# Contracting the 64-row products over 128 rows, with zeros in the others

## The chip, the cores and the metric

One core of a Trainium2 chip runs the whole step. The metric is the device time of one execution in microseconds (us). Engines are named as in the profile: PE (TensorE, its matmuls), PEld (its weight loads), DVE (VectorE), ACT (ScalarE), POOL (GpSimd), SP (SyncE, which issues nearly all DMAs).

## The reference

One layer over 2048 frames of a new stream (the prompt) and 64 frames of a running stream (the sample). An input projection feeds eight heads of banded attention and four heads of a gated linear recurrence; both are gated, joined, projected out and normalized. Cut to what the change touches:

```python
def sample_attention(q, k, v, ck, cv, rel_bias):      # 64 frames, 512 cached keys
    kk = jnp.concatenate([ck, k], axis=1)[:, None]    # 512 + 64 keys
    vv = jnp.concatenate([cv, v], axis=1)[:, None]
    ...
    return band_attention(q[:, None], kk, vv, rel, valid, rel_bias)[:, 0]

def band_attention(q, k, v, rel, valid, rel_bias):
    ...
    p = jax.nn.softmax(s, axis=-1).astype(v.dtype)
    return jnp.einsum('bnhqk,bnkhd->bnqhd', p, v)     # contracts over the keys

def step(S, inp):                                     # the recurrence, block by block
    ...
    A = jnp.where(mask, jnp.einsum('bthk,bshk->bhts', qt, kt), 0.0)
    o = jnp.einsum('bthk,bhkv->bthv', qt, S) + jnp.einsum('bhts,bshv->bthv', A, vb)
    S = jnp.exp(bl)[..., None] * S + jnp.einsum('bshk,bshv->bhkv', kb * jnp.exp(bl[:, None] - b), vb)
    return S, o
```

The sample has 64 frames. So its attention has 512 + 64 keys, and its recurrence has one chunk of 64 frames, where the prompt has chunks of 128.

## The kernel before

The frames are worked in four super-blocks (`SUPER`) of 512, 576, 512 and 512 columns; the second has the sample's 64 frames behind its 512 of the prompt. In each, PE runs 32 projections (`project`, tiles acc). Between their matmuls, in steps of two, the program lays the matmuls of the attention and of the recurrence as they become ready.

What sets the order: every engine is an in-order queue that the program fills itself. The class `Plan` keeps a clock of planned times; generators (threads) wait on planned times, on tokens for buffers (`tk`), or on conditions, and `mm`, `C.act`, `C.dve`, `C.pool` and `C.dma` advance the plan. What a generator emits between two waits goes to the engines' queues at that place.

Four heads pairs (`pair_jobs`, `attention`) handle the attention, two heads each. Keys lie on the partitions for the product with v: tile v has nine key tiles of 128 rows; the ninth (index 8) holds the sample's own 64 keys, in rows 0 to 63. For the sample, `sample_a` takes the scores, turns the probabilities to keys on partitions (tile tr), splits them into a high and a low part (tile ph, two buffers, `split_p`: ACT casts, DVE subtracts) and multiplies with v: for each of two heads four products over 128 cached keys (tile vc, in the buffer wraw) and one over the 64 last keys, j = 4.

The recurrence (`rec_block`, four heads) works in chunks of 128 rows, and of 64 for the sample (`chunks`, entry smp, two sub-blocks of 32). Of each chunk: A (tile asb, masked), kn (keys turned to frames on partitions, tile k1; for two heads of the later super-blocks by DMA, `by_dma`, L1518 to 1528, else by PE's transposes, L1530 to 1540), the products kv = kn with iv (L1545) and og = iv with A plus the state's part (L1580). iv is tile gi, [128, 640], filled by ACT from a DMA (`ev_i`); the sample's chunk is columns 512 to 639, rows 0 to 63. The last chunk's products contract over `w` = 64 rows.

Of float32 products (kv, og) each is two MATMUL instructions in the trace; the pv products take float32r tiles and are one each. All go through the helper `mm` (L249).

Of the kernel before, what the change touches and what calls it, by code (L numbers as in the profile page):

```python
# [17 lines left out]
P = 128  # L18
# [3 lines left out]
DEC = 64  # L22
WIN = 512
# [14 lines left out]
SUPER = [  # L38
# [4 lines left out]
]  # L43
# [140 lines left out]
def hymba_step(  # L184
# [26 lines left out]
    pool = nc.gpsimd  # L211
# [14 lines left out]
    def T(pool_, shape, dt, tag, **kw):  # L226
        uid[0] += 1
        return pool_.tile(list(shape), dt, tag=tag, name=f"{tag}_{uid[0]}", **kw)
# [13 lines left out]
    def f32(ap):  # L242
        return ap.bitcast(F32)
# [4 lines left out]
    def mm(out, w, x, n, slow=False, **kw):  # L248
        pe.matmul(out, w, x, **kw)  # L249
        C.mm(n, slow)  # L250

    def transpose(out, x, idn):
# [4 lines left out]
                                     w=WBUFS, raw=RAWB, xn=XNB, kv0=1, kv1=1, rec=1, sga=2, bias0=1, bias1=1, gf=1, gi=1, gg=1,  # L257
# [471 lines left out]
    room = {}  # L729
# [29 lines left out]
    def pair_jobs(sb, p):  # L759
# [12 lines left out]
        def open_(h):  # L772

            yield from tk[f"kv{h}"].get()
            if "kd" not in room:
                room["kd"] = T(pa, [P, 2, WIN + NMAX], F32R, "kd")
                room["v"] = T(pa, [P, 2, 9, 2, 64], F32R, "v")
                room["q"] = T(pa, [P, 2, QW], F32R, "q")
            d.kd, d.v, d.q = room["kd"], room["v"], room["q"]
            if sb:  # L780
                cd = carry[sb - 1][p]
                sp.dma_start(f32(d.kd[:, h, 0:512]), cd[:, h])
                d.k_t[h] = C.dma(256)
                sp.dma_start(f32(d.v[:, h, 0:4].rearrange("p t s d -> p (t s d)")), cd[:, 2 + h])
                d.v_t[h] = C.dma(256)
            d.open[h] = True
            C.spawn(load_bias(sb, p, d, h), 1)
# [185 lines left out]
    def vcols(v, t, h, rows):  # L973
        return (v[:rows, h, t] if v is room["v"] else v[:rows, t, 2 * h : 2 * h + 2, :]).rearrange("p s d -> p (s d)")

    def split_p(pt, ph, krows, wid, t):
        act.copy(ph[:krows, 0, :wid], pt[:krows, :wid])  # L977
        t = C.act(wid, t)
        yield "D", t
        dve.tensor_sub(ph[:krows, 1, :wid], pt[:krows, :wid], f32(ph[:krows, 0, :wid]))  # L980
        return C.dve(wid, t)
# [179 lines left out]
    def sample_a(d, c0, marks):  # L1161
        yield lambda: d.left == [1, 1]
        yield lambda: d.cache is not None and all(x >= c0 + DEC for x in d.q_n + d.k_n + d.v_n)
        yield "D", max(d.q_t + d.k_t + d.v_t)
        q, kd, v, p = d.q, d.kd, d.v, d.p
        kc, vc = d.cache


        spans = [(kc, 0, 512), (kd, 512 + c0, DEC)]

        z = c0 + DEC
        for part in (q, ql):
            dve.memset(f32(part[:, :, z : z + DEC]), 0.0)
            dve.tensor_copy(part[:, 1, z + DEC : z + 2 * DEC], f32(part[:, 1, c0:z]))
        t = C.dve(500)
        yield t
        yield from tk["s_ps"].get()
        yield from tk["pr"].get()
        sps = s_ps()
        for i, (ks, k0, kn) in enumerate(spans):  # L1180
            for part in (q, ql):
                for h in range(2):
                    a = (c0, z)[h]
                    mm(sps[:, i, :kn], part[:, h, a : a + P], ks[:, h, k0 : k0 + kn], kn,
                       start=part is q and h == 0, stop=part is ql and h == 1)
        t = C.pe()
        yield "D", t
        s = T(wk, [P, 640], F32, "pr", bufs=PRB)
        nm = T(wk, [P, 2], F32, "nm", bufs=4)
        for h in range(2):  # L1190
            hs = own[h]
            for i, kn in enumerate((512, DEC)):
                dve.tensor_tensor_reduce(s[hs, i * 512 : i * 512 + kn], sps[hs, i, :kn],
                                         d.bias[hs, h, 64 * h + i * 512 : 64 * h + i * 512 + kn],
                                         1.0, 3e38, ALU.add, ALU.min, nm[hs, i : i + 1])
                t = C.dve(kn, t)
        dve.tensor_tensor(nm[:, 0:1], nm[:, 0:1], nm[:, 1:2], ALU.min)
        t = C.dve(10, t)
        tk["s_ps"].put(1, t)
        for h in range(2):  # L1200
            d.left[h] -= 1
            tk[f"bias{h}"].put()
        yield "A", t
        out = []
        yield from softmax_exp(s, nm, 576, out, t)
        pr, t = out[0]
        yield lambda: marks[-1]["pv"] and turn["ph"] == turn["given"]
        yield t + 300.0
        phs = []
        for j0, nj, kr in ((0, 4, P), (4, 1, DEC)):  # L1210
            yield from tk["tr"].get()
            pt = tr_ps()
            for j in range(j0, j0 + nj):
                transpose(pt[:kr, (j - j0) * P : (j - j0 + 1) * P], pr[:, j * P : j * P + kr], ident)
            t = C.pe()
            if j0:
                tk["pr"].put(1, t)
            yield "A", t
            yield from tk["ph"].get()
            ph = T(wk, [P, 2, 512], F32R, "ph", bufs=2)  # L1220
            t = yield from split_p(pt, ph, kr, nj * P, t)
            tk["tr"].put(1, t)
            phs.append(ph)
        yield t + 200.0
        yield from tk["mixa"].get()
        mix = T(wk, [P, 256], F32, "mixa", bufs=2)
        yield from tk["pv"].get()
        pv = psum("pv").rearrange("p (h s q) -> p h s q", h=2, s=2)[:, :, :, :DEC]
        for h in range(2):
            for j in range(5):  # L1230
                kr = P if j < 4 else DEC
                cc = (j % 4) * P + h * DEC
                mm(pv[:, h], vcols(vc, j, h, kr) if j < 4 else vcols(v, 4 + c0 // P, h, kr), phs[j // 4][:kr, :, cc : cc + DEC], P,
                   start=(j == 0), stop=(j == 4))
        tk["ph"].put(2, C.pe())
        t = C.pe()
        yield "A", t
        for h in range(2):
            t = yield from finish_pv(h, pv[:, h], mix, DEC, t)
        tk["pv"].put(1, t)  # L1240
        tk["raw"].put(2)
        C.spawn(mix_out(d, mix, c0, DEC, t, True), 1)
# [5 lines left out]
    def head_jobs(sb, h):  # L1248
# [65 lines left out]
        def ifree():  # L1314
            if r.gi is None:
                if tk["gi"].n == 0:
                    return False
                tk["gi"].take()
                r.gi = True
                r.iv = T(pg, [P, 5 * P], F32, "gi")  # L1320
            return True

        def qd():
# [38 lines left out]
    def rec_block(r, off, bn, lastb):  # L1362
# [77 lines left out]
        A = asb  # L1440
# [75 lines left out]
        if by_dma:  # L1516
            yield ta + 200.0
            yield lambda: "t" in rows  # L1518
            yield rows["t"]
            kn = tmp("k1").rearrange("p (c t) -> p c t", t=P)  # L1520
            if nprc:
                act.copy(kn[:, :nprc].rearrange("p c (a j) -> p c a j", j=32),
                         kh[:, :full].rearrange("p (a c j) -> p c a j", a=4, j=32))
            if bn > full:
                act.copy(kn[:DEC, nprc], kh[:DEC, full : full + P])
            t = C.act(bn, rows["t"])
            yield t + 200.0
        else:
            yield max(ta, tkh) + 200.0
            tg = bank()  # L1530
            for i, (cc, nbk, smp) in enumerate(chunks):
                w = nbk * 32
                transpose(tg[:w, i], kh[:, cc : cc + w], ident)
            t = C.pe()
            yield "A", t
            kn = tmp("k1").rearrange("p (c t) -> p c t", t=P)
            for cs, w in merged():
                act.copy(kn[:w, cs], tg[:w, cs])
            t = C.act(bn, t)
            yield t + 200.0  # L1540
        kv = bank()
        iv = r.iv
        for i, (cc, nbk, smp) in enumerate(chunks):
            w = nbk * 32
            mm(kv[:, i], kn[:w, i], iv[:w, off + cc : off + cc + P], P, True, start=True, stop=True)  # L1545
        t = C.pe()
        yield "D", t
        before = []
# [28 lines left out]
        og = bank()  # L1577
        for i, (cc, nbk, smp) in enumerate(chunks):
            w = nbk * 32
            mm(og[:, i, :w], iv[:w, off + cc : off + cc + P], A[:w, i, :w], P, True,  # L1580
               start=True, stop=before[i] is None)
            if before[i] is not None:
                mm(og[:, i, :w], before[i], qh[:, cc : cc + w], P, True, start=False, stop=True)
# [673 lines left out]
```

## Time and profile before

| | |
|---|---|
| time, median of three runs | 1241.81 us (1240.01 to 1243.0) |
| the profiled execution's own time | 1241.93 us |
| its span, first to last instruction | 1240.2 us |
| mean granted clock of PE in it | 0.999 |
| instructions in it | 21233 |

How to read the rows that follow in the prediction. A group row has the line, engine, operation, tiles (out<-in, without buffer numbers), for PE the active rows*columns of the array, the shape and the count; then busy time in us, mean length of one in ns, and the engine's idle time ahead of them with what ended it. A timeline row has the start and length in us of a run of equal instructions, merged with their count. The ends of matmuls are modelled, so what a matmul holds PE for is read from one start to the next. A line of waits has the time in total, how often, and the longest.

### The profile page before, as it was taken

The page shows a single profiled execution, that of the slowest core. Times are in us where ns is not written, and L with a number is a line of the kernel's source. Part 1 is how long each engine was busy: PE and PEld are TensorE (multiplying, and loading weights), DVE is VectorE, ACT ScalarE, POOL GpSimd, SP SyncE. Part 2 cuts the span into 40 slices and gives each one's busy share as a digit, 9 for nine tenths or more (in the row PEclk, how much of TensorE's full clock was granted, in tenths as well). Part 3 has the DMA queues.
Part 4 walks back from the last instruction along what each step waited for, and adds up shares of the span by engine and source line. Part 5 has one row for each costly group of instructions (what it writes and reads, how often), then busy time and mean ns, then how long its engine had stood idle before and what let it go on. Part 6 is the DMA issues. An engine that isn't in the chain of part 4 may idle for free.

```text
span 1240.2 us, 21233 instructions
## 1 busy us (share of the span) xinstructions
PE 1228.5 (99%) x7398; PEld 1078.9 (87%) x7398; DVE 893.8 (72%) x1897; ACT 680.3 (55%) x1526; POOL 417.3 (34%) x702
## 2 busy tenths in 40 slices
PE   9999999999999999999999999999999999999997
PEld 7888888999999999998888888988888888788786
DVE  7687878777767677687587667785768566867775
ACT  6354546655565547574465556664646445644443
POOL 7665565111120111201242242133342202665543
PEclk9999999999999999999999999999999999999999
DMA  8897979667575476555787878678888686988431
GB/s 339 302 319 256 328 281 343 205 179 242 159 221 156 150 238 210 193 167 187 265 270 253 300 241 282 227 238 276 261 275 262 222 251 212 336 260 252 131 136 68
DMA packets 158324, 294.36 MB, mean 237 GB/s; under 512 B 51657, under 2 KB 98377, under 8 KB 140554
## 3 DMA queue, kind: packets, MB, share of 16 engines
q1 hardware_dynamic: 157784, 292.74, 70.7%
q8 instruction: 58, 0.95, 0.3%
q14 instruction: 48, 0.39, 0.1%
q10 hardware_dynamic: 434, 0.27, 0.1%
HBM read 198.52 MB, written 95.49 MB: 237 GB/s over the span
## 4 chain that ended last, share of the span: by engine, by line
PE 90%; DMA 5%; DVE 2%; ACT 1%; SPq 1%; issue 0%; POOL 0%; ACTq 0%; DVEq 0%; POOLq 0%
PE acc L249 58%; PE g L249 9%; PE pv L249 7%; PE tr L253 6%; PE s L249 5%; PE tr L249 4%; DMA vT<-way 2%; DMA w<-wd 2%; DMA way<-vT 1%; DMA out_dram<-ck 1%; PE g L253 1%; DMA bias<-wind 0%; DVE pr L948 0%; SPq L711 0%; SPq L1684 0%
## 5 line engine op out<-in xcount | busy, mean ns | idle before, releaser
L249 PE MATMUL acc<-xh,w 128*128 128x512 f32 (+2 forms) x2720 | 564.5, 347 | 0.6 <-ACT xh L409 0.5
L249 PEld LDWEIGHTS acc<-xh,w 128*128 128x128 f32 x2720 | 435.7, 189 | 51.5 <-ACT xh L409 0.9
L249 PE MATMUL acc<-xl,w 128*128 128x512 f32 (+2 forms) x1360 | 291.4, 346 | 0.2 <-DVE xl L415 0.2
L249 PEld LDWEIGHTS acc<-xl,w 128*128 128x128 f32 x1360 | 220.5, 189 | 26.2 <-DVE xl L415 0.4
L948 DVE CUSTOM_DVE_ANT_0 pr<-s,bias 128x640 f32<-128x640 f32 (+4 forms) x128 | 94.2, 736 | 53.6 <-PE s L249 53.1
L965 ACT ACTIVATE pr<-pr,nm 128x640 f32<-128x640 f32 (+4 forms) x132 | 100.3, 760 | 52.8 <-DVE nm L948 52.5
L977 ACT CAST ph<-tr 128x512 fp32r<-128x512 f32 (+3 forms) x176 | 87.8, 506 | 74.5 <-PE pv L249 45.5
L473 POOL TENSOR_TENSOR w<-wraw,w 128x256 fp32r<-128x256 f32 x120 | 102.3, 881 | 55.6 <-DVE w L468 40.5
L980 DVE TENSOR_TENSOR ph<-tr,ph 128x512 fp32r<-128x512 f32 (+3 forms) x176 | 100.7, 587 | 21.6 <-ACT ph L977 21.0
L249 PE MATMUL pv<-ph,v 128*128 128x256 f32 (+2 forms) x344 | 97.8, 371 | 0.9 <-DVE ph L980 0.6
L253 PE MATMUL tr<-ident,pr 128*128 128x128 f32 x580 | 88.2, 273 | 0.5 <-DVE sm L968 0.5
L1596 POOL TENSOR_TENSOR k<-ob 128x512 f32<-128x512 f32 (+2 forms) x20 | 18.0, 902 | 200.3 <-ACT ob L1587 162.3
L510 POOL TENSOR_TENSOR xn<-wraw,xn 128x256 fp32r<-128x256 f32 x48 | 40.6, 848 | 132.1 <-ACT xn L507 127.1
L1121 POOL TENSOR_TENSOR mixa<-mixa,sga 128x256 f32<-128x256 f32 (+1 forms) x36 | 28.6, 793 | 167.9 <-DVE mixa L1019 142.2
L969 DVE TENSOR_SCALAR pr<-pr,sm 128x640 f32<-128x640 f32 (+4 forms) x132 | 76.2, 577 | 4.7
L1019 DVE TENSOR_TENSOR mixa<-mixa,pv 64x256 f32<-64x256 f32 (+1 forms) x144 | 56.8, 394 | 31.0 <-ACT mixa L1015 27.3
L253 PEld LDWEIGHTS tr<-ident,pr 128*128 128x128 f32 x580 | 69.8, 140 | 10.3 <-PE tr L253 0.9
L575 ACT ACTIVATE sig<-acc 128x512 f32<-128x512 f32 (+2 forms) x63 | 31.8, 505 | 72.8 <-PE acc L249 72.1
L249 PEld LDWEIGHTS pv<-ph,v 128*128 128x128 f32 (+1 forms) x344 | 58.2, 189 | 9.8 <-DVE ph L980 1.4
L1015 ACT COPY mixa<-pv 64x256 f32<-64x256 f32 (+1 forms) x72 | 25.1, 349 | 59.4 <-PE pv L249 53.3
L249 PE MATMUL s<-kd,q 128*128 128x320 f32 (+2 forms) x232 | 55.8, 311 | 0.2 <-DVE nm L948 0.2
L249 PE MATMUL s<-kd,ql 128*128 128x320 f32 (+2 forms) x232 | 55.5, 309 | 0.0
(415 smaller groups left out, 2122.5 us busy)
## 6 DMA issues: line engine op xcount, KB each, us to landing
w<-wd SPq DMA_DIRECT2D x96, 1024.0 KB, 5.8
wd<-w SPq DMA_DIRECT2D x32, 1024.0 KB, 7.4
wraw<-in_w_in_dram SPq DMA_DIRECT2D x30, 512.0 KB, 5.4
wod<-xn SPq DMA_DIRECT2D x28, 512.0 KB, 5.8
xn<-in_x_prompt_dram SPq DMA_DIRECT2D x23, 512.0 KB, 4.8
bias<-biasd SPq DMA_DIRECT2D x24, 320.0 KB, 5.5
carry<-kd SPq DMA_DIRECT2D x12, 512.0 KB, 6.2
carry<-v SPq DMA_DIRECT2D x12, 512.0 KB, 6.4
```

The source lines that it names most:

```text
L249: pe.matmul(out, w, x, **kw)
L253: pe.transpose(out, x, idn)
L473: pool.tensor_sub(w[:, 1, k : k + 2], raw[:, k : k + 2], f32(w[:, 0, k : k + 2]))
L510: pool.tensor_sub(f32r(st[:, c.start + 512 : c.stop + 512]), src[:, c], st[:, c])
L575: act.activation(sig[:, :bn], acc, AF.Exp, scale=-1.0)
L948: dve.tensor_tensor_reduce(s[:, :nk].rearrange("p (a c) -> p a c", a=ns), sps[:, :ns, :kn], d.bias[:, h, bcol : bcol + nk].rearrange("p (a ...
L965: act.activation(s[:, :nk], s[:, :nk], AF.Exp, bias=nm[:, 0:1], scale=-1.0, accum_out=sm)
L969: dve.tensor_scalar(s[:, :nk], s[:, :nk], sm, None, ALU.mult)
L977: act.copy(ph[:krows, 0, :wid], pt[:krows, :wid])
L980: dve.tensor_sub(ph[:krows, 1, :wid], pt[:krows, :wid], f32(ph[:krows, 0, :wid]))
L1019: dve.tensor_add(mix[hs, :qn], mix[hs, :qn], pv[hs, i, :qn])
L1121: pool.tensor_mul(mix[:, :n], mix[:, :n], d.sg[:, g0 : g0 + n])
```

## The change

Every product that contracted over 64 rows now contracts over 128. The 64 further rows of one operand or both are cleared by memsets on POOL: those of v's ninth key tile once, when the tile is first made; those of ph for each pair of the sample; those of iv's last chunk for each head of the second super-block; those of kn's last chunk likewise. A needs none: its tile asb is zero from the start, and the masked copies leave these rows as they are. The transposes of 64 rows (L253) stay.

```diff
@@ open_ (pair_jobs)
                 room["v"] = T(pa, [P, 2, 9, 2, 64], F32R, "v")
+                pool.memset(f32(room["v"][DEC:, :, 8]), 0.0)
@@ sample_a
             ph = T(wk, [P, 2, 512], F32R, "ph", bufs=2)
+            if kr < P:
+                pool.memset(f32(ph[kr:, :, : nj * P]), 0.0)
             t = yield from split_p(pt, ph, kr, nj * P, t)
...
             for j in range(5):
-                kr = P if j < 4 else DEC
                 cc = (j % 4) * P + h * DEC
-                mm(pv[:, h], vcols(vc, j, h, kr) if j < 4 else vcols(v, 4 + c0 // P, h, kr), phs[j // 4][:kr, :, cc : cc + DEC], P,
+                mm(pv[:, h], vcols(vc, j, h, P) if j < 4 else vcols(v, 4 + c0 // P, h, P), phs[j // 4][:, :, cc : cc + DEC], P,
                    start=(j == 0), stop=(j == 4))
@@ ifree (head_jobs)
                 r.iv = T(pg, [P, 5 * P], F32, "gi")
+                if SUPER[sb][1] > WIN:
+                    pool.memset(r.iv[DEC:, WIN : WIN + P], 0.0)
@@ rec_block
             if bn > full:
                 act.copy(kn[:DEC, nprc], kh[:DEC, full : full + P])
+                pool.memset(kn[DEC:, nprc], 0.0)
...
             for cs, w in merged():
                 act.copy(kn[:w, cs], tg[:w, cs])
+                if w < P:
+                    pool.memset(kn[w:, cs], 0.0)
...
-            mm(kv[:, i], kn[:w, i], iv[:w, off + cc : off + cc + P], P, True, start=True, stop=True)
+            mm(kv[:, i], kn[:, i], iv[:, off + cc : off + cc + P], P, True, start=True, stop=True)
...
-            mm(og[:, i, :w], iv[:w, off + cc : off + cc + P], A[:w, i, :w], P, True,
+            mm(og[:, i, :w], iv[:, off + cc : off + cc + P], A[:, i, :w], P, True,
                start=True, stop=before[i] is None)
```

The plan's clock isn't advanced for the memsets, so PE, DVE, ACT and SP get their instructions in the same order as before; only POOL's queue has 13 more. Two places of it follow; the names are out<-in with buffer numbers, which differ between the two programs. The first is the second pair's sample attention in the second super-block, POOL before:

```order
L1121 TENSOR_TENSOR mixa_4875<-mixa_4875,sga_4428 128x256
L1596 TENSOR_TENSOR k_1076_5499<-ob_5495 128x256
L1121 TENSOR_TENSOR mixa_5132<-mixa_5132,sga_4428 128x256
L1618 TENSOR_TENSOR ob_5495<-ob_5495,gg_5335 128x256
L1121 TENSOR_TENSOR mixa_5538<-mixa_5538,sga_4428 128x64
```

And the same place on POOL now:

```order
L1434 COPY fk_5245<-eb_5167 128x2
L1324 MEMSET gi_5311 64x128
L1122 TENSOR_TENSOR mixa_4881<-mixa_4881,sga_4433 128x256
L1223 MEMSET ph_5514 64x2x128
L1603 TENSOR_TENSOR k_1076_5506<-ob_5502 128x256
L1122 TENSOR_TENSOR mixa_5138<-mixa_5138,sga_4433 128x256
L1625 TENSOR_TENSOR ob_5502<-ob_5502,gg_5342 128x256
L1122 TENSOR_TENSOR mixa_5546<-mixa_5546,sga_4433 128x64
```

The clearing of gi stands ahead of the first mixa, and that of ph between mixa and k<-ob, the square of ob for a recurrence head's norm. The second place is the recurrence of the third head, its last block in the second super-block, POOL before:

```order
L1433 COPY pf_5652<-eb_5615 128x1
L1434 COPY sf_5653<-eb_5615 128x1
L1435 TENSOR_TENSOR et_5654<-eb_5615 128x1
L1596 TENSOR_TENSOR k_1152_5934<-ob_5930 128x320
L1618 TENSOR_TENSOR ob_5930<-ob_5930,gg_5335 128x320
```

And now:

```order
L1437 COPY pf_5660<-eb_5623 128x1
L1438 COPY sf_5661<-eb_5623 128x1
L1439 TENSOR_TENSOR et_5662<-eb_5623 128x1
L1545 MEMSET k_1120_5798 64x128
L1603 TENSOR_TENSOR k_1152_5943<-ob_5939 128x320
L1625 TENSOR_TENSOR ob_5939<-ob_5939,gg_5342 128x320
```

The clearing of kn (here k_1120) stands behind the small factors of this block and ahead of the same block's k<-ob. On PE the product of the last keys with v and the product kv now wait for POOL as well; lines from about 780 on are two to seven higher than before.

## The prediction

> **What bounds the kernel now.** I read the page first (busy shares and clock), then busy time by stretch, then TensorE's waits, then its groups by shape, then its timeline around the products that change.
>
> ```profile
> span 1240.2 us, 21233 instructions
> PE 1228.5 (99%) x7398; PEld 1078.9 (87%) x7398; DVE 893.8 (72%) x1897; ACT 680.3 (55%) x1526; POOL 417.3 (34%) x702
> ...
> 300.00:600.00 300.00, 300.00 (x2200) 285.53 (x2200) 215.02 (x565) 172.76 (x421) 40.02 (x126) 1.00 0.58 184
> ...
> PE acc L249 <- DMA w<-wod: 1.1, 1, 1.1
> ```
>
> TensorE is the bound: busy 99% of the span. The third row is the stretch from 300 to 600 us, in which the second super-block's attention and recurrence run: after the length come busy time and instructions of PE, PEld, DVE, ACT and POOL, then the granted clock, 1.00. PE is busy for all 300.00 of 300.00 us and POOL for 40.02. The last row is the longest of PE's waits past the start, 1.1 us once; it lies at 1065.90 (its row is below). So what a PE instruction costs from its start to the next start is paid in full, and a shorter one is gained in full, if nothing else becomes late.
>
> The products of 64 rows are these (rows*columns of the array that are active stand ahead of the shape):
>
> ```profile
> L249 PE MATMUL pv<-ph,v 64*128 64x128 f32 x8 | 2.6, 324 | 0.0
> L249 PE MATMUL g<-gi,k 64*128 64x128 f32 x8 | 1.9, 323 | 0.0
> L249 PE MATMUL g<-asb,gi 64*128 64x64 f32 x8 | 1.7, 296 | 0.0
> ```
>
> 24 instructions: per pair two of the last keys (h = 0, 1, j = 4 at L1233), per head one product kv (L1545) and one og (L1580), each of two instructions. Means of 296 to 324 ns are lengths with a modelled end; the price is in the starts.
>
> **What a full-height product costs.** The timeline (start, length, form and count) of a stretch in which all rows are 128 high:
>
> ```profile
> 783.95 0.39 PE L249 MATMUL g<-asb,gi 128*128 128x128 f32 x2
> ...
> 785.51 0.39 PE L249 MATMUL g<-bm,S 128*128 128x128 f32 x2
> ```
>
> From 783.95 to 785.51 fourteen instructions start, 1.56 us: **0.111 us each**. Full-height instructions that stream 64 columns (g<-bm,So, below) are taken at 0.111 too: their pair needs 0.28 from 460.66 to 460.94, right behind a change of height, which is 0.06 over two of 0.111.
>
> **The change, part 1: PE.** Three places, one of each kind; the other pairs and heads show the same steps.
>
> ```profile
> 432.84 0.64 PE L249 MATMUL acc<-xh,w 128*128 128x256 f32 x4
> 433.31 0.56 PE L249 MATMUL pv<-ph,wraw 128*128 128x128 f32 x4
> 433.80 0.32 PE L249 MATMUL pv<-ph,v 64*128 64x128 f32 x1
> 434.06 0.66 PE L249 MATMUL pv<-ph,wraw 128*128 128x128 f32 x4
> 434.65 0.32 PE L249 MATMUL pv<-ph,v 64*128 64x128 f32 x1
> 434.90 0.74 PE L249 MATMUL acc<-xh,w 128*128 128x256 f32 x4
> 435.48 0.76 PE L249 MATMUL acc<-xl,w 128*128 128x256 f32 x5
> ```
>
> Last keys: ten pv instructions take 434.90 - 433.31 = 1.59 us; at 0.111 they take 1.11, so 0.48 is lost. The four acc behind them take 435.48 - 434.90 = 0.58, the same four ahead 433.31 - 432.84 = 0.47: 0.11 more is lost where PE comes back to full height. 0.59 per pair, four pairs: **2.36 us**.
>
> ```profile
> 450.96 1.02 PE L249 MATMUL g<-gi,k 128*128 128x128 f32 x6
> 451.92 0.56 PE L249 MATMUL s<-kd,q 128*128 128x320 f32 x2
> 452.31 0.45 PE L249 MATMUL s<-kd,ql 128*128 128x320 f32 x2
> 452.60 1.12 PE L249 MATMUL acc<-xl,w 128*128 128x256 f32 x8
> ```
>
> kv: the row of six merges four full and the two 64-row instructions. 451.92 - 450.96 = 0.96 against 6 x 0.111 = 0.67: 0.29. The scores behind take 0.39 for two, the next two 0.29: 0.10. 0.39 per head: **1.56 us**.
>
> ```profile
> 459.99 0.39 PE L249 MATMUL g<-bm,S 128*128 128x128 f32 x2
> 460.30 0.43 PE L249 MATMUL g<-asb,gi 64*128 64x64 f32 x2
> 460.66 0.43 PE L249 MATMUL g<-bm,So 128*128 128x64 f32 x2
> 460.94 1.05 PE L253 MATMUL tr<-ident,pr 128*128 128x128 f32 x8
> ```
>
> og: six instructions from 459.99 to 460.94, 0.95 against 0.67: 0.28 per head, **1.12 us**. Sum 2.36 + 1.56 + 1.12 = **5.04 us**. The changed products all take forms that the trace has already, so the price is bounded closely: at best a run of pv begins with a short step, as here (the first four are 0.56 long, of which the last one's own length is about 0.39 - 0.11 = 0.28, so three steps take 0.28 and not 0.33), 0.05 per pair, 5.2 in all; at worst only the slower step of the 64-row instruction goes and the slower step of its neighbours stays. That is 0.14 of the 0.25 at 433.80, twice in each pair, and about 0.15 of 0.36 for the two at 460.30 and as much for kv: 4 x (0.28 + 0.15 + 0.15) = 2.3. I take 5.0, since the step into 64 rows (0.31 at 459.99 against 0.22 for a pair of full ones) belongs to the change of height and there is no such change left.
>
> ```profile
> L249 PEld LDWEIGHTS pv<-ph,v 128*128 128x128 f32 x336 | 56.8, 189 | 9.3 <-DVE ph L980 1.4 <-issue 0.6 <-DVE v L683 0.6
> L249 PEld LDWEIGHTS pv<-ph,v 64*128 64x128 f32 x8 | 1.5, 183 | 0.6
> ```
>
> A weight load of 64 rows takes 183 ns, one of 128 rows 189. The Trainium skill speaks against this change: "TensorE: Matmul & The Clock Gate", section "LDWEIGHTS (loading the stationary operand)", has the load follow the columns and not the contraction, and its table "Why this matters for your kernels" gives a matmul of few rows alone the same time as a full one; by it the sum would be 0, a rival below. The load rows agree, the start-to-start rows don't: they show 0.25 where full ones show 0.111. Another page of the Trainium skill, "TensorEngine Tiling (Array Packing)", section "Key Properties", says that changing the tiling mode drains the engine; by it the sum is the 5.0 above.
>
> **Part 2: POOL.** Thirteen memsets are added: one of v, four each of gi, kn and ph. PE, DVE, ACT and SP keep their order.
>
> ```profile
> L281 POOL MEMSET asb<- 128x128 f32 x1 | 0.2, 204 | 0.0
> L288 POOL MEMSET asb<- 128x512 f32 x1 | 0.5, 524 | 0.0
> ...
> 40.28 1.43 POOL L473 TENSOR_TENSOR w<-wraw,w 128x256 fp32r<-128x256 f32 x2 [2.22 <-issue]
> ...
> 429.54 0.61 POOL L1596 TENSOR_TENSOR k<-ob 128x256 f32<-128x256 f32 x1 [5.53 <-ACT ob L1587]
> ...
> 508.13 0.74 POOL L1618 TENSOR_TENSOR ob<-ob,gg 128x256 f32<-128x256 f32 x1 [3.05 <-DVE ob L1614]
> ...
> 511.45 0.32 PE L249 MATMUL pv<-ph,v 64*128 64x128 f32 x1
> ...
> 428.76 0.48 PE L249 MATMUL pv<-ph,v 128*128 128x256 f32 x2
> ...
> 431.72 0.40 PE L249 MATMUL g<-q,ones 128*128 128x256 f32 x2
> ...
> 449.62 0.53 ACT L1538 COPY k<-g 128x256 f32<-128x256 f32 x2 [3.51 <-PE g L253]
> ```
>
> 128 elements per partition took 204 ns, 512 took 524: 0.83 ns per element more. The eight of 128 elements (gi, kn) I take at 0.20, the five of 256 (v, ph) at 0.31: 3.2 us of POOL in all, between 0.10 and 0.52 each by the smallest and largest near rows. What hides them:
> - v, once, in the first super-block: the row at 40.28 shows POOL idle for 2.22 us right behind the place. Without that cover it delays one split of weights by 0.31.
> - gi: waits for PE to have read the head before's. Its product comes behind a DMA and an ACT copy into the same tile, both longer than a memset.
> - kn: waits for PE's last product with k1. ACT's copy into the same tile waits for that and for PE's transposes behind it, and starts at 449.62; the product is at 450.96, so 0.20 fits with 1.1 us to spare or more.
> - ph: waits for PE's last product with the old buffer, as ACT's cast of the new one does already; a DVE subtraction follows the cast. It is tightest in pair 2 (counted from 0), where POOL works on ob to 508.87: cleared by 509.2, used at 511.45, 2.2 us to spare.
>
> Queued behind a ph memset are mixa (its DMA isn't urgent) and, in pairs 1 and 3, k<-ob, for which DVE waits and then PE (g<-q,ones). In pair 1 the buffer is free when the pv at 428.76 end, at 429.24, so the memset ends near 429.6 and k<-ob starts 0.1 late; its consumer on PE at 431.72 comes 1.5 us after k<-ob ends. So part 2 costs **0**, with at most 8 x 0.5 = 4 us if every cleared operand came just too late.
>
> **Sum.** The profiled execution took 1241.93 us (span 1240.2 and 1.7 around it), 0.1 above the median of 1241.81. 1241.9 - 5.0 = **1236.9 us**.
>
> **The rivals.**
> - *Part of the gain comes back as a wait at the end* (chance 0.08). Between 300 and 600 us PE waits for nothing; the longest wait is here:
>
> ```profile
> 1065.90 2.12 PE L249 MATMUL acc<-w,slot 128*128 128x512 f32 x8 [1.08 <-DMA w<-wod]
> ...
> 1054.91 0.92 SPq L2117 DMA_DIRECT2D w<-wod  x2
> ...
> SPq L446 <- PE acc L249: 199.1, 61, 10.7
> ```
>
> If that transfer, issued at 1054.91, were held by the DMA queue and not by PE, PE would wait up to 5.0 longer: 1241.9, at half 1239.4. Against it: w's loads wait for PE to release a buffer (the third row: 61 such waits), so they move up with PE.
> - *The surcharge doesn't belong to the height* (0.04) but to the new weight tile or the last product of a group: 1241.9. Against it: g<-asb,gi at 783.95 and at 460.30 are the same tiles at the same place of the chunk's work, in full and in half height, and a pair takes 0.22 there and 0.36 here. The page on TensorE that is named above (the Trainium skill) would have it so.
> - *Slower: PE waits for POOL* (0.03). Place: the product of the last keys and kv, which now wait for the clearing at L1223, L1530 or L1545. Eight such waits; from 5.0 / 8 = 0.63 us of lateness each the gain is gone, and with one step like ob (0.74) ahead in the queue at the wrong moment and the memset's 0.31, 1.05 us each, it is 1241.9 - 5.0 + 8.4 = 1245.3. Against it: the spare time above, 1.1 us at the least.
>
> **How the numbers follow.** Forecast 0.85: 1236.9. About 0.2% (2.5 us) is what a measurement of this kernel can tell from no change, so faster means below 1239.3. The forecast and a third of the first rival lie there: 0.87. Same: the rest of the first, the second: 0.10. Slower: 0.03. The range goes from 1235.0 (5.2 gained, and 1.7 for the spread of the three runs, 1240.0 to 1243.0) to 1240.2 (half the gain handed back, or the low bound 2.3 of part 1, with some of that spread).
>
> **What would show it.** Right: no 64-row row of pv, g<-gi,k or g<-asb,gi; ten pv instructions in 1.1 us; PE busy near 1223.5 at 99%; POOL near 420.5 with 715 instructions; PE's list of waits without POOL beyond the start. Wrong: steps of 0.2 or more inside these stretches (the height wasn't it), a wait PE pv or g <- POOL (third rival), or a longer wait for w<-wod (first).

## The result, and the profile after

| | before | after |
|---|---|---|
| time, median (lowest to highest, runs) | 1241.53 us (1240.01 to 1243.0, 6) | 1236.69 us (1236.22 to 1237.89, 6) |
| ratio after / before, 95% interval | | 0.9961 (0.995 to 0.9971) |
| the profiled execution | 1241.93 us | 1236.36 us |
| its span | 1240.2 us | 1234.6 us |

The forecast was 1236.9. The change is worth 4.8 us of 1241.5, a little under half a percent, and the interval of the ratio excludes 1.

The page of the kernel after (span and busy time of each engine), then its busy time by stretch for 300 to 600 us, columns as in the row of before, then the head of TensorE's list of waits:

```profile
span 1234.6 us, 21261 instructions
PE 1223.1 (99%) x7398; PEld 1076.8 (87%) x7398; DVE 896.2 (73%) x1897; ACT 680.2 (55%) x1526; POOL 421.7 (34%) x715
...
300.00:600.00 300.00, 300.00 (x2223) 287.53 (x2223) 216.39 (x571) 176.00 (x428) 43.77 (x138) 1.00 0.60 188
...
PE pv L2060 <- POOL one L279: 1.4, 1, 1.4
PE acc L249 <- DVE gq L580: 0.8, 1, 0.8
PE tr L253 <- DVE sm L969: 0.5, 1, 0.5
PE acc L249 <- ACT xh L409: 0.5, 1, 0.5
PE pv L249 <- DVE ph L981: 0.4, 1, 0.4
PE acc L249 <- DMA w<-wod: 0.4, 1, 0.4
```

TensorE has the same 7398 instructions and is 5.4 us less busy; it still never waits between 300 and 600 us, and in those 300 us it starts 23 instructions more than before. POOL has 13 instructions and 4.4 us more, of which the memsets are 3.1 (their rows are below). The list holds no wait for POOL except one at line 2060, which the list of before has too (line 2053, also 1.4 us).

The groups by shape, after. No row of pv, of g<-gi,k or of g<-asb,gi with 64 rows is left; the three rows of 64 that remain are transposes. The same view has the memsets on POOL:

```profile
L249 PE MATMUL g<-asb,gi 128*128 128x64 f32 x8 | 1.3, 248 | 0.0
L253 PE MATMUL tr<-ident,vT 64*128 64x64 f32 x8 | 0.9, 235 | 0.0
L253 PE MATMUL tr<-ident,xn 64*128 64x64 f32 x4 | 0.5, 235 | 0.0
L253 PE MATMUL g<-ident,xn 64*128 64x64 f32 x4 | 0.5, 234 | 0.0
...
L1223 POOL MEMSET ph<- 64x256 f32 x4 | 1.2, 308 | 18.2 <-PE pv L249 18.1
L1324 POOL MEMSET gi<- 64x128 f32 x4 | 0.8, 201 | 0.2
L1530 POOL MEMSET k<- 64x128 f32 x2 | 0.4, 200 | 7.6 <-PE g L249 7.6
L1545 POOL MEMSET k<- 64x128 f32 x2 | 0.4, 200 | 8.5 <-PE g L249 8.5
L778 POOL MEMSET v<- 64x256 f32 x1 | 0.3, 309 | 0.1
```

0.20 and 0.31 us, as estimated from the two rows of asb. TensorE's timeline at the three places that the prediction worked out: pair 1's last keys, head 2's kv, and head 2's og.

```profile
431.91 0.56 PE L249 MATMUL pv<-ph,wraw 128*128 128x128 f32 x4
432.31 0.27 PE L249 MATMUL pv<-ph,v 128*128 128x128 f32 x1
432.42 0.61 PE L249 MATMUL pv<-ph,wraw 128*128 128x128 f32 x4
432.87 0.28 PE L249 MATMUL pv<-ph,v 128*128 128x128 f32 x1
432.98 0.69 PE L249 MATMUL acc<-xh,w 128*128 128x256 f32 x4
433.50 0.76 PE L249 MATMUL acc<-xl,w 128*128 128x256 f32 x5
...
448.99 0.83 PE L249 MATMUL g<-gi,k 128*128 128x128 f32 x6
449.58 0.54 PE L249 MATMUL s<-kd,q 128*128 128x320 f32 x2
449.95 0.45 PE L249 MATMUL s<-kd,ql 128*128 128x320 f32 x2
...
457.63 0.39 PE L249 MATMUL g<-bm,S 128*128 128x128 f32 x2
457.85 0.33 PE L249 MATMUL g<-asb,gi 128*128 128x64 f32 x2
458.02 0.39 PE L249 MATMUL g<-bm,So 128*128 128x64 f32 x2
458.25 0.94 PE L253 MATMUL tr<-ident,pr 128*128 128x128 f32 x7
```

From the first pv to the second run of acc: 1.59 us, before 2.17 (433.31 to 435.48). From kv to the second pair of scores: 0.96, before 1.35. From g<-bm,S to the transposes: 0.62, before 0.95. That is 0.58, 0.39 and 0.33 us, where 0.59, 0.39 and 0.28 were expected.

Both traces have TensorE's 7398 matmuls in the same order, so each start of after can be set against its start of before. This table is worked out so from the two traces (before minus after, from each span's start; the gain up to that time):

```
at us      240    300    400    500    600    700   1060   1080   end
gain us   0.12  -0.55   1.40   2.69   4.52   4.50   4.66   5.56   5.60
```

Between 300 and 600 us, where all the changed products lie (before, from 302.48 to 599.6), 5.07 us is gained. The rest is two waits that have nothing to do with the changed products: 0.68 us is lost at 258 us (a wait for DVE's gq, the second row of waits above), and about 0.9 is won from 1060 to 1080, where the wait for w<-wod took 1.1 us before and 0.4 after. Below, "gain of the stretch" is this difference between 300 and 600 us of one profiled execution each. Waits elsewhere scatter by about as much as the parts to be told apart, and the stretch leaves them out.

### The profile page after: what moved, and what is told of

Same layout as the page of the kernel before. It is cut to its first block, busy times and chain, and to the rows that moved or that the text cites. A ratio compares the mean times of both kernels' runs of the same rounds, so it can differ in the third digit from the quotient of the medians.

```text
span 1234.6 us, 21261 instructions
## 1 busy us (share of the span) xinstructions
PE 1223.1 (99%) x7398; PEld 1076.8 (87%) x7398; DVE 896.2 (73%) x1897; ACT 680.2 (55%) x1526; POOL 421.7 (34%) x715
## 4 chain that ended last, share of the span: by engine, by line
PE 93%; DVE 3%; DMA 2%; ACT 1%; issue 0%; SPq 0%; POOL 0%; DVEq 0%; POOLq 0%
PE acc L249 61%; PE g L249 9%; PE pv L249 7%; PE tr L253 6%; PE s L249 5%; PE tr L249 4%; DMA way<-vT 1%; DMA out_dram<-sig 1%; PE g L253 1%; DMA w<-wd 0%; DMA sig<-mixd 0%; DVE xl L415 0%; DVE pr L970 0%; DMA vT<-way 0%; ACT ck L368 0%
## 5 line engine op out<-in xcount | busy, mean ns | idle before, releaser
L249 PE MATMUL acc<-xl,w 128*128 128x512 f32 (+2 forms) x1360 | 291.3, 346 | 0.4 <-DVE xl L415 0.4
L253 PE MATMUL tr<-ident,pr 128*128 128x128 f32 x580 | 88.3, 273 | 0.7 <-DVE sm L969 0.5
L253 PEld LDWEIGHTS tr<-ident,pr 128*128 128x128 f32 x580 | 69.6, 140 | 11.0 <-DVE ph L981 1.2
L249 PEld LDWEIGHTS pv<-ph,v 128*128 128x128 f32 x344 | 58.4, 189 | 8.1 <-DVE ph L981 1.2
```

The source lines that it names most:

```text
L253: pe.transpose(out, x, idn)
```

## The experiments

The theory: what costs is the change of the active height between two neighbouring products, not the height. The rivals: 64-row products are slow by themselves; the surcharge belongs to the place of these products; clearing on POOL is paid for. Each ratio is to runs of the kernel before on the same chip (medians 1241.61 for the first four kernels, 1242.04 for the fives, the fourteen and the wide A, 1242.0 for five and eight clears).

### Clears alone

The kernel after, with the products over 64 rows as before; the 13 memsets stay.

```diff
-                mm(pv[:, h], vcols(vc, j, h, P) if j < 4 else vcols(v, 4 + c0 // P, h, P), phs[j // 4][:, :, cc : cc + DEC], P,
+                kr = P if j < 4 else DEC
+                mm(pv[:, h], vcols(vc, j, h, kr) if j < 4 else vcols(v, 4 + c0 // P, h, kr), phs[j // 4][:kr, :, cc : cc + DEC], P,
...
-            mm(kv[:, i], kn[:, i], iv[:, off + cc : off + cc + P], P, True, start=True, stop=True)
+            mm(kv[:, i], kn[:w, i], iv[:w, off + cc : off + cc + P], P, True, start=True, stop=True)
...
-            mm(og[:, i, :w], iv[:, off + cc : off + cc + P], A[:, i, :w], P, True,
+            mm(og[:, i, :w], iv[:w, off + cc : off + cc + P], A[:w, i, :w], P, True,
```

> The thirteen memsets of the change on POOL, and every product as before (64 rows). The height theory (PE loses time where it goes into and out of 64 rows; the memsets are hidden): 1241.5 us, no change, and the three 64-row groups as before. The theory that the memsets themselves moved the time, or that the gain is a shift of waits: 1237 to 1240 us.

Measured 1241.74 us, ratio 0.9999 (0.9991 to 1.0008); gain of the stretch 0.00 us. The memsets by themselves cost nothing and bring nothing.

### The keys alone, the recurrence alone

The first has kv and og as before, without the memsets of gi and k1; the second has pv as before, without the memsets of v and ph. Lines of the second's edit:

```diff
-                pool.memset(f32(room["v"][DEC:, :, 8]), 0.0)
...
-                pool.memset(f32(ph[kr:, :, : nj * P]), 0.0)
```

> Only the last keys of the sample's attention over 128 rows, with the clearing of v and ph; kv and og as before. Height theory: 4 x 0.58 = 2.3 us less than before, 1239.2 us. If one of the two parts carries everything: 1241.5 or 1236.7 us.

> Only kv and og over 128 rows, with the clearing of gi and kn; the last keys as before. Height theory: 4 x (0.39 + 0.33) = 2.9 us less than before, 1238.6 us. If one of the two parts carries everything: 1241.5 or 1236.7 us.

Measured 1238.89 us, 0.998 (0.9969 to 0.999), and 1238.83 us, 0.9975 (0.9966 to 0.9984). Gain of the stretch: 2.30 and 2.77 us. Together 5.07, which is that of the whole change: the parts add up, and neither takes from the other. The prediction's terms were 2.36 and 1.56 + 1.12 = 2.68; the expectation of the second run had 2.9, from 0.39 for kv in each head and the 0.33 of og that the kernel after had shown.

### The two 64-row products next to each other

The kernel before, with the order of the ten pv of a pair turned so that the first head's last-key product stands right ahead of the second's. As many 64-row products, half as many changes of height.

```diff
-            for j in range(5):
+            for j in ((0, 1, 2, 3, 4), (4, 0, 1, 2, 3))[h]:
...
-                   start=(j == 0), stop=(j == 4))
+                   start=(j == (0, 4)[h]), stop=(j == (4, 3)[h]))
```

> The kernel before with the sample's ten products of a pair in another order: the two of 64 rows stand next to each other (head 0: j = 0 to 4, head 1: j = 4, 0 to 3), nothing cleared, nothing made higher. Height theory: PE goes into 64 rows once per pair and not twice, so of the 0.58 lost per pair about half, 0.25 to 0.3, goes: 1.0 to 1.2 us less than before, 1240.4 us, and ten pv instructions take about 1.3 and not 1.59 us. Theory that a 64-row product is slow by itself (0.25 where a full one takes 0.111): no change, 1241.5 us, and the two adjacent ones start 0.25 apart.

Measured 1240.74 us, 0.9996 (0.9987 to 1.0005): by the time alone not to be told from before. The trace tells it: gain of the stretch 1.15 us. Its timeline at pair 1:

```profile
432.86 0.56 PE L249 MATMUL pv<-ph,wraw 128*128 128x128 f32 x4
433.35 0.44 PE L249 MATMUL pv<-ph,v 64*128 64x128 f32 x2
433.71 0.55 PE L249 MATMUL pv<-ph,wraw 128*128 128x128 f32 x3
```

The two take 0.36 us together (433.35 to 433.71), where in the kernel before one took 0.26 and 0.25. This kernel has four round trips between the heights less than before, each 1.15 / 4 = 0.29 us.

### Five times the last keys

The kernel before, and the kernel after, each with the last-key product done five times in a row for each head (so that these keys count five times).

```diff
-            for j in range(5):
+            for n, j in enumerate((0, 1, 2, 3, 4, 4, 4, 4, 4)):
...
-                   start=(j == 0), stop=(j == 4))
+                   start=(n == 0), stop=(n == 8))
```

> The kernel before with the product of the last keys made five times in a row instead of once (the sum counts these keys five times, so the sample's attention is another): 32 more 64-row products, none of them a new change of height. Height theory: they cost as much as full ones, 0.11 each, 3.6 us: 1245.1 us, and in a run of five the three in the middle start 0.11 apart. Theory that a 64-row product is slow by itself (0.25): 8.0 us, 1249.6 us.

> The changed kernel with the same: the product of the last keys five times in a row, over 128 rows, with zeros in the others (the sample's attention as in the run before). Both theories: 32 x 0.11 = 3.6 us over the changed kernel, 1240.3 us. What tells is the distance to five_times: 4.9 us by the height theory, as without the repeats; 9 us or more if each 64-row product is slow.

Measured 1245.98 us, 1.0036 (1.0023 to 1.005), with 64 rows, and 1242.16 us, 1.0001 (0.9989 to 1.0013), with 128. The second lies 1.9 above its expectation, and its runs reach from 1239.4 to 1246.2; its profiled execution took 1240.58. Half a microsecond of the 1.9 may be the chip (the kernel before took 1242.04 on it, and 1241.53 on the one from which the expectation was worked out); the rest isn't explained. The distance is 3.8 us in medians and 5.1 in spans (1244.0 and 1238.9), and matmul against matmul, from 300 to 700 us, 5.07: with 32 more 64-row products on one side, what full height is worth is the same. Were the low product slow by itself, the distance would have gone to 9 or more. Pair 1 with 64 rows (timeline of the run over 64 rows):

```profile
433.50 0.56 PE L249 MATMUL pv<-ph,wraw 128*128 128x128 f32 x4
433.99 0.77 PE L249 MATMUL pv<-ph,v 64*128 64x128 f32 x5
434.69 0.66 PE L249 MATMUL pv<-ph,wraw 128*128 128x128 f32 x4
435.29 0.77 PE L249 MATMUL pv<-ph,v 64*128 64x128 f32 x5
435.99 0.74 PE L249 MATMUL acc<-xh,w 128*128 128x256 f32 x4
```

Five low products take 0.70 us (433.99 to 434.69). The steps from one start to the next in ns, worked out from the traces of four kernels at this pair, from the first pv on; 64-row products in brackets, the last numbers are the acc behind:

```
before      62 113 110 205 [255] 163 112 113 203 [254] | 222 119
after       61 114 109 115  109  114 108 115 110  114  | 169 121
adjacent    62 113 109 206 [165   201] 163 113 110 112 | 170 118
five times  61 114 109 206 [165 111 110 112 203] 164 113 109 206 [165 112 110 111 204] | 222 118
```

Inside a run of these 64-row products the step is 110 to 112 ns, that of a full one. What is long is the last step ahead of a change of height, in either direction (200 to 206, 0.09 us more), and the first behind it (163 to 165, 0.05 more). A single 64-row product between full ones has both, 255, and gives the full ones at its sides 205 and 163: 0.28 us for a round trip.

The transposes that stay at 64 rows show the same. They come in four runs of four, and the steps of such a run in the kernel after are 111 to 114, 61 to 63 twice, and 152 to 154 ns: the first 0.05 and the last 0.09 over those between. No run removes these changes of height.

The products kv and og fit less well. They come only in twos, and in the kernel before the step from the first 64-row instruction of a two to the second is 213 ns for kv and 160 for og, where the kernel after has 112 and 59: 0.10 more, twice the 0.05 above. There is no longer run of them, so whether the other 0.05, some 0.4 us in the eight twos, belongs to the change or to the low product itself stays open.

### The clears made longer

The kernel after, with each of the four ph clears done fourteen times, to find out when they are late.

```diff
-                pool.memset(f32(ph[kr:, :, : nj * P]), 0.0)
+                for _ in range(14):
+                    pool.memset(f32(ph[kr:, :, : nj * P]), 0.0)
```

> The changed kernel with each clearing of ph made 14 times in a row on POOL, so that it ends about 4 us later. It had 3.3, 4.1, 2.1 and 2.6 us to spare. If PE waits for the clearing as soon as the spare time is gone (the third rival's mechanism), PE shows waits for POOL of about 0.7, 0, 1.9 and 1.5 us: 1240.8 us. If the spare time is larger than the trace says or the wait is not on PE's path: 1236.7 us.

Measured 1253.03 us, 1.0088 (1.0075 to 1.0102): 16 us over the kernel after, and both expected times were missed. The first two lines of TensorE's waits, then the timeline of POOL at pair 2 and that of TensorE at pairs 1 and 2, then stretches of 2 to 5 us behind the waits at pairs 1, 2 and 3 (length, PE busy and instructions, granted clock, DMA):

```profile
PE pv L249 <- POOL ph L1224: 5.8, 3, 2.5
PE g L249 <- DVE q L1607: 3.6, 1, 3.6
...
512.04 5.04 POOL L1224 MEMSET ph<- 64x256 f32 x14
...
434.64 0.58 PE L249 MATMUL g<-q,ones 128*128 128x256 f32 x1 [3.60 <-DVE q L1607]
...
517.13 0.47 PE L249 MATMUL pv<-ph,v 128*128 128x128 f32 x1 [2.50 <-POOL ph L1224]
517.41 1.05 PE L249 MATMUL pv<-ph,wraw 128*128 128x128 f32 x4
...
435.00:438.00 3.00, 3.00 (x14) 0.50 0.30 33
438.00:440.00 2.00, 2.00 (x18) 1.00 0.65 217
517.00:522.00 5.00, 4.87 (x22) 0.50 0.51 103
609.00:612.00 3.00, 3.00 (x9) 0.50 0.41 57
```

Three things had been left out. Fourteen clears take 5.04 us, so one more costs 0.364 and not its own length of 0.307; they end 4.73 us later, and the product waits 2.5 us at pair 2, 2.1 at pair 3 and 1.3 at pair 0, where 1.9, 1.5 and 0.7 were expected. At pair 1 what waits is g<-q,ones: its operand q waits on DVE for k<-ob, which stands behind the clears on POOL (3.6 us). And at each of the waits of 2.1 us and more, or within a microsecond behind it, TensorE's granted clock falls to 0.50, by the trace's record of the clock for 3.41 us from 434.57, 6.83 from 516.49 and 3.41 from 608.65; at pair 0, with its 1.3, it stays at 1.00. At 0.50 the four pv from 517.41 are 1.05 us long, where 0.61 is usual. Matmul against matmul with the kernel after, the stretch loses 16.2 us: 10.1 at the four products that wait (3.75, 2.66, 2.23 and 1.45, each 0.1 to 0.2 more than the wait that the profile lists), and 6.1 behind them, of which 5.9 at the low clock.

On that clock the Trainium skill, "TensorE: Matmul & The Clock Gate", section "Part 1: The HAM clock gate (the "warmup" mystery)", says that the array runs at half its clock after an idle window of about 3.4 us, and at full again after about as long a busy one. This trace agrees on the half and, with 3.41 us twice, on the way back (once it was 6.83); waits of 2.1 and 2.5 us, shorter than that window, were enough here.

Two smaller doses were to show whether short waits have that price too, and where the spare time ends: five and eight clears (the diff is the same with 5 and 8).

> The kernel after with each of the four clears of ph done five times. In the run with fourteen, 14 clears took 5.04 us (512.04 to 517.08), so one more costs POOL 0.364 us; four more are 1.46 us. The spare times in the changed kernel's trace are 3.3, 4.1, 2.1 and 2.6 us, so if the clears are hidden by spare time of POOL no pv product waits. Behind pair 1's clear stands k<-ob (line 1603), for which DVE's q and then TensorE's g<-q,ones wait; there 4.73 us more became a wait of 3.75, so about 1.0 us is spare and 0.5 us would be waited: 1237.2. If the clears' time counted in full once the engine is kept busy, 4 x 1.46 = 5.8 more: 1242.5.

> The same with each clear done eight times: 2.55 us more each. Pair 2 is then late by 2.55 - 2.12 = 0.4 us, g<-q,ones behind pair 1's clear by 2.55 - 1.0 = 1.6 us, pairs 0 and 3 not at all: 2.0 us of waits. With fourteen, waits of 3.75, 2.66 and 2.23 us were followed by stretches at a granted clock of 0.65 to 0.86 that cost 6.0 us more, and a wait of 1.45 us by none. If only long waits are followed by a lower clock, 1236.7 + 2.0 = 1238.7. If every wait is, in proportion to its length (6.0 us on 10.1), 1239.9.

Measured 1237.71 us, 0.9962 (0.995 to 0.9974), and 1239.97 us, 0.9981 (0.9972 to 0.9991). The stretch loses 0.61 us against the kernel after with five, 2.3 with eight. For the run with eight, two rows of TensorE's waits, the timeline at pair 2, and the stretch behind the longer wait:

```profile
PE g L249 <- DVE q L1607: 1.4, 1, 1.4
...
PE pv L249 <- POOL ph L1224: 0.3, 1, 0.3
...
511.78 0.33 PE L249 MATMUL pv<-ph,v 128*128 128x128 f32 x1 [0.33 <-POOL ph L1224]
...
434.00:439.00 5.00, 5.00 (x43) 5.00 (x42) 4.45 (x12) 4.03 (x12) 2.74 (x9) 1.00 0.64 220
```

With five clears no product waits for ph; with eight the one of pair 2 does, by 0.3 us. The first to suffer is g<-q,ones, with a listed wait of 0.3 us with five and 1.4 with eight. The expectations were worked out from starts set against starts; so measured, g<-q,ones is 0.49 us late with five (0.5 expected) and 1.58 with eight (1.6), and the product of pair 2 is 0.49 late (0.4). The clock is 1.00 from 300 to 600 us: here waits of this size cost themselves and no more. The time alone doesn't decide between 1238.7 and the rival's 1239.9: 1239.97 is 3.3 over the kernel after, or 2.8 if each is set against the kernel before on its own chip. But the stretch accounts for 2.3 of it, 2.07 at the two late products, and at 1.00 none of the rest is the clock behind these waits; in the trace it lies ahead of 300 and behind 600 us.

### The sample's A at full width

Could something further be had in the same way? In the kernel after, the sample's product A takes 64 columns of k0 and stands behind products of 128 columns; here it takes 128, the further ones cleared on POOL.

```diff
+        if bn % P:
+            pool.memset(k0[:, bn : bn + DEC], 0.0)
...
-            mm(ag[:w, i, :w], k0[:, cc : cc + w], q0[:, cc : cc + w], w, True, start=True, stop=True)
+            mm(ag[:, i, :w], k0[:, cc : cc + P], q0[:, cc : cc + w], w, True, start=True, stop=True)
```

> The changed kernel, and the sample's product for A takes 128 columns of k0 instead of 64 (POOL clears the 64 further ones, the result's further rows are not read): PE then doesn't leave the full width for it. If a change of width costs what a change of height does: about 0.23 for each of four heads, 0.9 us less, 1235.8 us. If only the height costs: 1236.7 us.

Measured 1236.32 us (1234.72 to 1237.63, five runs), 0.9955 (0.9943 to 0.9967) of before. Against the kernel after its stretch gains 0.64 us. The stretch holds only three of the four products: that of the first head starts at 291.3 us, ahead of it. Set start against start, each of the four gains 0.23 us, 0.91 in all, which is the 0.9 expected. The steps in ns at the second head, from the last product of 128 columns on (A's two in brackets, then two of what follows):

```
after    205 [107 152] 222 209
wide A   111 [ 59  84] 202 210
```

So a change of width has a price of this kind too: 0.09 us on the step ahead of it, and the rest on A's own two steps and the one behind. What of A's own steps belongs to the change and what to the narrow product itself, these two don't tell apart. The time doesn't show the gain safely: 0.4 us below the kernel after, or 0.9 if each is set against the kernel before on its own chip, with intervals that overlap. So no version is shown by its time to be faster than the kernel after.

## Why the prediction was right, step by step

- **TensorE is the bound, and a shorter step is gained in full.** Right: it waits for nothing in the stretch, before and after, and the shorter steps at the changed places, 5.1 us added up one by one, are 5.07 us of earlier starts over the stretch; the lead of 4.5 us at 600 is still 4.3 to 4.7 up to 1060.
- **Last keys, 0.59 a pair.** Right: 0.58. The keys alone gave 2.30 us for the 2.36 of four pairs.
- **kv, 0.39 a head.** Right at the head that was worked out, 0.39, and at two others (0.39 and 0.40), but not at the first: there a transpose stands behind kv and 0.31 was gained. That the other heads show the same steps was wrong for this one; the term of 1.56 is 1.48.
- **og, 0.28 a head.** Too small: 0.33. The step that was off is the full-height pair with 64 columns, taken at 0.111 us an instruction; g<-asb,gi over 128 rows takes 0.17 for two (457.85 to 458.02). The prediction had argued from the pair g<-bm,So, 0.28 from 460.66 to 460.94; that was long because of the change of height ahead of it and is 0.23 now. The term of 1.12 is 1.34. The recurrence alone gave 2.77 against the 2.68 of kv and og. That the sum is met so closely, 5.04 predicted and 5.07 found, is in part luck: og was 0.2 too small, kv and the last keys together 0.15 too large.
- **The surcharge belongs to the change of height, so the neighbours' long steps go too.** Right, and shown by the runs, since before's trace could not tell it from the low bound of 2.3: two low products side by side save one round trip, and further low products cost a full product's step. These runs are of the last keys' product; for kv and og it is shown that the whole surcharge goes at full height, and not that all of it is the change's.
- **POOL's clears cost 0.** Right: nothing by themselves, and with the products changed the stretch gains the whole sum. The spare time at the tightest ph, put at 2.2 us, is 2.1: cleared by 506.55, used at 508.67. The 1.5 us that k<-ob behind pair 1's clear was given as spare are 1.0 by the longer clears (with fourteen, 4.73 us later and the product 3.75 late; with five 1.46 and 0.49, with eight 2.55 and 1.58), because DVE's work on q, 0.42 us, lies in between and had not been taken off. It is the smallest spare that the runs measured: there, and not at the product that uses ph, lateness would first have been paid.

Of the rivals, *the gain comes back as a wait for w<-wod* did not come: that wait fell from 1.1 to 0.4 us, and as it was 1.6 with five clears it says little either way. *The surcharge isn't the height's*, with the time unchanged at 1241.9, falls by the time of the kernel after. *PE waits for POOL* needed lateness that didn't exist. Its price, the wait's own length, would have held at 1.05 us a wait, as it did for the 1.4 with eight clears; the waits of 2.1 us and more with fourteen cost more than their length.

The page of the Trainium skill that stood behind the second rival ("TensorE: Matmul & The Clock Gate", the table "Why this matters for your kernels") gives a product of few rows alone the time of a full one. The traces agree for a 64-row product of the last keys among its like, with a step of 110 to 112 ns; the 0.25 of a single one is the change of height at its two sides. The Trainium skill, "TensorEngine Tiling (Array Packing)", section "Key Properties", says that a change of tiling mode drains the engine. The traces don't show a drain as such; they show 0.14 us for each change between 64 and 128 rows at these products.

## What to carry to other kernels

A few small products among large ones can cost as much in the steps of their neighbours as in their own: compare the start-to-start steps of the instruction ahead and of the one behind with those of an undisturbed run, and either give the odd ones their neighbours' shape or lay them side by side. Filling up with zeros is free only while the clearing engine has time to spare, and the tightest place may be a later instruction in its queue, not the cleared tile. For an effect of half a percent and its parts, matching the instructions of two traces one by one shows within one stretch what the medians can hardly separate; the stretch has to hold all the changed instructions.

## What the runs showed of the hardware that was not expected

- Between products of 128 and of 64 active rows, the step ahead of the change was 0.09 us longer and the one behind it 0.05, in both directions alike at the products of the last keys (200 to 206 and 163 to 165 ns, where 109 to 115 are usual). At kv and og the step behind the change into 64 rows was 0.10 longer.
- Between products of 128 and of 64 active columns, the step ahead of the change was 0.09 us longer (205 ns against 111), and a pair of narrow products cost 0.23 us in all.
- TensorE's granted clock fell to 0.50 for 3.4 to 6.8 us at waits of 2.1 to 3.6 us (three of three), and not at waits of 1.3 and 1.4 us: with fourteen clears 6.1 us were lost behind 10.1 us of waits. Five waits are too few to say where between 1.4 and 2.1 us this begins, or whether it always does.
- Fourteen equal memsets of 64x256 in a row came every 0.364 us, while each is listed with 0.307.
